# A two-layer trunk on one core: masks and gates in another memory, modulation sums taken earlier, four pooled products moved in TensorE's order, and the first attention biases loaded during a feed-forward product

## The chip, the core and the metric

The kernel runs as one program on one core of a Trainium2 chip. The metric is the device time of one execution in microseconds (us). A core has five engines with a queue each: TensorE (PE, matmuls; its weight loads are listed as PEld), VectorE (DVE), ScalarE (ACT), GpSimd (POOL) and SyncE (SP), which issues all the transfers of this kernel. An engine works through its queue in order, and an instruction whose operand isn't ready holds up everything behind it on its engine.

## The reference

512 tokens of 1024 features go through two layers of two steps each; a step is x + gate * norm(fn(norm(x) * (1 + scale) + shift)). The three modulation vectors of a step come from silu(c) times a matrix (`ada_w`).

```python
def sandwich(x, mod, g_pre, g_post, fn):
    shift, scale, gate = mod
    h = rms_norm(x, g_pre) * (1.0 + scale[:, None]) + shift[:, None]
    return x + gate[:, None] * rms_norm(fn(h), g_post)
...
for layer in range(DEPTH):
    # layer 0: pooling and the HGRN recurrence; layer 1: dilated attention with a position bias
    x = sandwich(x, modulation(...), ..., mixer)
    x = sandwich(x, modulation(...), ..., lambda h: (silu(h @ w_a) * (h @ w_b)) @ w_out)
```

The mixer of layer 0 has two halves. The pooling half takes `u = h @ w_u` in four groups of 128 features, subtracts `u` from a running mean over 2, 4, 8 or 16 tokens, and multiplies each group by a 128x128 matrix. The HGRN half (4 heads of 128) is a gated linear recurrence over the tokens; its output is normed and multiplied by `silu(h @ w_g)`. Layer 1's attention has 24 heads in three groups, and a bias that depends on the distance of two tokens.

## The kernel before

**Arithmetic.** Every large product is made of three fp32r passes: an operand is split into a high part (`hi`, a copy by ACT, line 353 for weights and 572 for the other operand) and a low part (`lo`, a subtraction by DVE or POOL, line 286), and PE adds hi·hi, hi·lo and lo·hi (line 265, function `mm`). A weight block is 128x1024 numbers, 512 KB.

**Memory.** On-chip memory is shared out in units of 512 numbers per partition by an `Arena` each for plain data (`ar`: a zone "f" of 24 units, of which x holds 8), for temporaries (`tr`: zone "t", 8 units) and for split operands (`rr`: "r" and "o"). Two further "swing" zones, "s" and "z", belong to `ar` in the mixer and in attention and to `rr` elsewhere. The zone "o" of 4 units holds the split operands of the feed-forward output product. `get(n, zone)` takes n units of a zone, `free` gives them back; a transfer into freed units waits until their last reader is done.

**Loads.** All weight blocks stand in one list. `weights(i)` makes sure that block i is split, splits up to `ahead["split"]` blocks beyond it, and issues loads up to `ahead["load"]` blocks beyond it, as long as more than `ahead["f"]` units (and 2 for the block) of zone "f" are free. While a half is interleaved with other work (`busy`) there is no splitting ahead except where the table `ENDS` asks for it.

**Order.** PE's order is that of the program text (`hold(pe)`); in some stretches ACT, DVE, POOL and SP are held to it too, elsewhere a scheduler chooses their order when the program is built. One instruction of the modulation sums (line 405) multiplies a 128x1025 tile of `ada_w` (512.5 KB, three buffers) by silu(c) and sums it; an `ada_step` is two of them. There are 48 steps; a step's number is counted in `ada["at"]`, and the steps 8 to 19 belong to the mixer's stage.

**Stages.** Times are those of the profiled execution.

- Start (0 to 57 us): norm of x, products with `w_qf`. PE is given some products of zeros (`keep_warm`, counts in `WARM`) while it waits.
- Values (57 to about 107): `values_block(kk)`, with the first levels of the recurrence.
- Pool and gates (107 to 168): in PE's order `mixed(g)` (u), `pooled(g)` (the 128x128 product of group g, three passes, whose operand comes from `means(g)` on DVE and a split), `blocks_64`, `blocks_128` (parts of the recurrence inside 64 or 128 tokens), `gate(h)` (24 passes of 128x512 each), `keys_back`, `states`, `outputs`.
- Mixer's output product (168 to 241): `out_project(0, ...)`, in halves of 256 tokens; `between(i)` puts the rest of the recurrence (`gated_head`, `states`, `outputs`) between its blocks.
- Feed-forward of layer 0, `ffn(1, ...)` (241 to about 630): `project_head`, the rest of the 44 blocks of `w_fi`, then `out_project` over the 22 blocks of `w_fo`. Its blocks 0 to 14 are done for all 512 tokens (48 passes each), the last 7 (`tail = ENDS[1][0]`), 15 to 21, first for one half of the tokens and then for the other (24 passes each), so that the first half's norm runs beside the second half's products. `operand(i, hf)` splits the block's other operand into zone "o"; ACT and DVE can start on it once PE has read what stood there.
- Attention (from about 630), feed-forward of layer 1, output.

The 6 transfers of `load_biases(pair)` bring a pair's biases, written to memory in the mixer, into 3 units of `ar`; those of pair 0 are issued at the start of attention.

Of the kernel before, what the change touches and what calls it, by code (L numbers as in the profile page):

```python
# [51 lines left out]
WARM = 9, 5, 7  # L52
# [3 lines left out]
ADA = 12, 16  # L56
# [123 lines left out]
def trunk(ctx: ExitStack, tc: tile.TileContext, a: dict, out: bass.AP, last: int = 3):  # L180
# [275 lines left out]
    for i, b in enumerate(c_banks):  # L456
        mm(b, bk[b], small[0:1, 0:1].broadcast_to([1, P]), c_row[:, i * T : (i + 1) * T], True, True)
    warm_r = ar.get(1)
    warm = ar.ap(warm_r, P)
    pool.memset(warm, 0.0)  # L460

# [60 lines left out]
    masks_r = ar.get(3)  # L522
    masks = ar.ap(masks_r).bitcast(I32).rearrange("p (l c) -> p l c", l=6)
    for k in range(ND):
# [21 lines left out]
        if k == 6:  # L546
            sp.dma_start(ar.ap(masks_r), a["masks"])
# [215 lines left out]
    def out_project(s, base, n, srcs, ada_until, late=None):  # L763
# [79 lines left out]
        for i in range(n - tail):  # L843
# [7 lines left out]
            rr.free(g[0])  # L851
        hold(pe, act, dve, pool)
# [66 lines left out]
    acc_r = [ar.get(1) for _ in range(1)]  # L919
    accs = [ar.ap(acc_r[0])[:, pr * 256 : (pr + 1) * 256] for pr in range(2)]  # L920
    A_r = [ar.get(2, "s") for _ in range(2)]
    A = [ar.ap(r).rearrange("p (n t) -> p n t", n=8) for r in A_r]
    pool.memset(ar.ap(acc_r[0]), 0.0)
# [68 lines left out]
    if last >= 2:  # L992
        vec_r = biases()

# [137 lines left out]
    def gate(h):  # L1132
        b = bk.get()
        project(w_g + h, b)
        g_rs0.append(ar.get(1, "f"))
        act.activation(ar.ap(g_rs0[h]), bk[b], AF.Silu)
# [6 lines left out]
    def keys_back(h):  # L1143
        pr, hh = divmod(h, 2)
        if h < 2:
            kst_rs.append(tr.get(1))
            S_rs.append(tr.get(1))
# [4 lines left out]
        act.activation(tr.ap(kst_rs[h % 2], 3 * P), bk[b][:, 0 : 3 * P], AF.Copy)  # L1152
        bk.free(b)

    def states(h):

        pr, hh = divmod(h, 2)
        kst, S = tr.ap(kst_rs[h % 2], 3 * P), tr.ap(S_rs[h % 2], 3 * P)
# [14 lines left out]
    def outputs(h):  # L1173
        pr, hh = divmod(h, 2)
        S, ob = tr.ap(S_rs[h % 2], 3 * P), ob_of[h]
# [14 lines left out]
    def gated_head(h):  # L1190
# [7 lines left out]
        dve.scalar_tensor_tensor(ar.ap(y_r), bk[b], ogain, ar.ap(g_rs0[h]), ALU.mult, ALU.mult)  # L1198
# [13 lines left out]
    ar.free(acc_r[0])  # L1212
    ar.free(masks_r)
# [3 lines left out]
    pooled(1)  # L1217
    ahead.update(load=9, split=4, f=4)
    gate(0)
    both(blocks_128)  # L1220
# [5 lines left out]
    pooled(2)  # L1226
# [4 lines left out]
    pooled(3)  # L1231
    rr.free(pwh_r)
    rr.free(pwl_r)
# [12 lines left out]
    keys_back(3)  # L1246
    ada_step(ADA[1])
    out_banks = [bk.get() for _ in range(4)]

    def between(i):  # L1250
# [6 lines left out]
        elif i == 2:  # L1257
            outputs(2)
            outputs(3)
            swing_to(ar, rr)  # L1260
# [3 lines left out]
        if i < 4:  # L1264
            ada_step(20)

    def end_of_mixer():
        release()
        for r in (*qp_r, *ks_r, *A_r, v_r, *g_rs0):
            ar.free(r)  # L1270
        for r in (*t_regions, *kst_rs, *S_rs):
# [11 lines left out]
    def ffn(s, layer, ada_until, chain):  # L1283
# [31 lines left out]
        ahead.update(load=14, split=14, f=2, r=4)  # L1315
# [8 lines left out]
    def attention(s, chain):  # L1324
# [20 lines left out]
        for i in range(N_QK):  # L1345
            r = ar.get(1)
# [7 lines left out]
        biases_of = {}  # L1354

        def load_biases(pair):
            r = ar.get(3)
# [325 lines left out]
```

## Time and profile before

| what | before |
|---|---|
| median of 3 runs (lowest to highest) | 1270.33 us (1269.47 to 1273.18) |
| profiled execution, its time and its span | 1271.72 us, 1269.9 us |
| PE busy | 1231.6 us (97%) |
| DVE, ACT, POOL busy | 620.5, 461.7, 194.7 us |
| mean granted TensorE clock | 0.988 |
| transfers | 164.25 MB, mean 129 GB/s |

The span runs from the first to the last instruction; the time of the execution is a little longer. A row of the timeline gives start and duration, engine, line, operation, output and input, and in brackets how long the engine had been idle before it and what released it. PE's rows overlap by a fraction of a microsecond, since matmuls are pipelined; the distance between the starts of two rows is what counts.

### The profile page before, as it was taken

What the parts mean: (1) busy time and instruction counts of PE and PEld (TensorE: products, weight loads), DVE (VectorE), ACT (ScalarE), POOL (GpSimd) and SP (SyncE); (2) the same over time, 40 slices, a digit from 0 to 9 for tenths busy, and PEclk for the clock granted to TensorE, in tenths of its full rate; (3) what the DMA queues carried; (4) which work ended last, traced back from release to release, by engine and by line L of the source; (5) the groups of instructions that cost most, each with busy time, mean ns of one, the idle gap of its engine ahead of it and who ended that gap; (6) DMA issues with size and microseconds to landing.
All of it is one profiled execution on the core that took longest, in us unless ns stands there. A gap on an engine that the chain in (4) does not pass through costs nothing.

```text
span 1269.9 us, 20632 instructions
## 1 busy us (share of the span) xinstructions
PE 1231.6 (97%) x8672; PEld 1091.6 (86%) x8672; DVE 620.5 (49%) x974; ACT 461.7 (36%) x757; POOL 194.7 (15%) x110
## 2 busy tenths in 40 slices
PE   8999899999999999999999999999999999999997
PEld 6777699988888889998979878778998888889997
DVE  7978966754443223528485232455854222213415
ACT  4553445532222222326453233445732222222313
POOL 1000022321111111213211110022311111121002
PEclk9999899999999999999999999999999999999999
DMA  8943732336552133321378222123435222223302
GB/s 308 351 147 130 271 127 87 135 128 222 193 195 76 67 100 100 128 89 54 116 251 287 78 71 75 54 95 119 134 127 188 83 83 67 68 99 100 100 1 67
DMA packets 50383, 164.25 MB, mean 129 GB/s; under 512 B 5809, under 2 KB 11081, under 8 KB 50290
## 3 DMA queue, kind: packets, MB, share of 16 engines
q1 hardware_dynamic: 50290, 162.93, 37.8%
q8 instruction: 68, 1.11, 0.4%
q14 instruction: 25, 0.20, 0.0%
HBM read 160.78 MB, written 2.13 MB: 128 GB/s over the span
## 4 chain that ended last, share of the span: by engine, by line
PE 84%; DVE 7%; DMA 3%; ACT 2%; issue 2%; POOL 1%; SPq 0%; DVEq 0%; ACTq 0%; POOLq 0%
PE bank L265 81%; DMA ada_w<-ada 2%; DVE ada_w L405 1%; DVE r L286 1%; PE bank L1475 1%; DVE t L649 1%; PE bank L1444 1%; DVE f L653 1%; DMA f<-w_qf 1%; DVE h L688 0%; DVE t L610 0%; POOL h L286 0%; PE bank L936 0%; POOL cst L481 0%; DMA f<-w_ho 0%
## 5 line engine op out<-in xcount | busy, mean ns | idle before, releaser
L265 PE MATMUL bank<-h,r 128*128 128x512 f32 (+1 forms) x2096 | 457.5, 360 | 1.5 <-ACT h L529 0.7
L265 PEld LDWEIGHTS bank<-h,r 128*128 128x128 f32 x2096 | 358.9, 189 | 61.5 <-ACT h L529 2.0
L265 PE MATMUL bank<-h,swing 128*128 128x512 f32 (+1 forms) x1688 | 325.3, 341 | 1.2 <-DVE swing L1298 1.2
L265 PEld LDWEIGHTS bank<-h,swing 128*128 128x128 f32 x1688 | 269.9, 189 | 37.3 <-DVE swing L1298 1.4
L286 DVE TENSOR_TENSOR r<-f,r 128x1024 fp32r<-128x1024 f32 (+1 forms) x67 | 81.6, 1220 | 181.4 <-PE bank L265 98.5
L353 ACT ACTIVATE r<-f 128x1024 fp32r<-128x1024 f32 x105 | 110.3, 1058 | 140.3 <-PE bank L265 107.0
L265 PE MATMUL bank<-o,swing 128*128 128x256 f32 x1248 | 152.0, 275 | 0.0
L265 PEld LDWEIGHTS bank<-o,swing 128*128 128x128 f32 x1248 | 146.3, 188 | 0.1
L286 DVE TENSOR_TENSOR swing<-f,swing 128x1024 fp32r<-128x1024 f32 x49 | 66.3, 1357 | 133.4 <-PE bank L265 81.0
L405 DVE SCALAR_TENSOR_TENSOR ada_w<-ada_w,sil 128x1025 f32<-128x1025 f32 x96 | 126.2, 1328 | 10.3 <-DMA ada_w<-ada 9.2
L353 ACT ACTIVATE swing<-f 128x1024 fp32r<-128x1024 f32 x80 | 83.5, 1058 | 93.9 <-PE bank L265 51.5
L286 POOL TENSOR_TENSOR r<-f,r 128x1024 fp32r<-128x1024 f32 x24 | 58.7, 2445 | 323.6 <-PE bank L265 243.7
L265 PE MATMUL bank<-o,r 128*128 128x256 f32 x864 | 107.4, 276 | 0.0
L265 PEld LDWEIGHTS bank<-o,r 128*128 128x128 f32 x864 | 102.6, 188 | 0.2
L1297 ACT ACTIVATE t<-bank 128x512 f32<-128x512 f32 (+1 forms) x52 | 27.2, 531 | 176.2 <-PE bank L265 176.0
L286 POOL TENSOR_TENSOR swing<-f,swing 128x1024 fp32r<-128x1024 f32 x23 | 56.6, 2460 | 215.2 <-PE bank L265 175.5
L265 PE MATMUL bank<-h,o 128*128 128x512 f32 (+1 forms) x296 | 78.2, 350 | 1.7 <-DVE h L688 1.7
L265 PE MATMUL bank<-r,h 128*128 128x512 f32 x288 | 73.4, 404 | 0.6 <-ACT swing L907 0.6
L265 PEld LDWEIGHTS bank<-r,h 128*128 128x128 f32 x288 | 62.5, 252 | 8.1 <-ACT swing L913 1.2
L286 DVE TENSOR_TENSOR o<-f,o 128x256 fp32r<-128x256 f32 (+2 forms) x38 | 26.6, 717 | 73.7 <-ACT o L572 66.8
L265 PEld LDWEIGHTS bank<-h,o 128*128 128x128 f32 x296 | 52.6, 190 | 10.0 <-DVE h L688 2.1
L481 POOL TENSOR_TENSOR cst<-cst 128x2 f32<-128x2 f32 (+1 forms) x19 | 16.9, 891 | 275.8 <-DVE cst L479 275.8
(189 smaller groups left out, 1005.9 us busy)
## 6 DMA issues: line engine op xcount, KB each, us to landing
ada_w<-ada SPq DMA_DIRECT2D x96, 512.5 KB, 4.7
f<-w_fi SPq DMA_DIRECT2D x88, 512.0 KB, 4.5
f<-w_fo SPq DMA_DIRECT2D x44, 512.0 KB, 3.4
f<-w_aqk SPq DMA_DIRECT2D x24, 512.0 KB, 4.5
f<-w_av SPq DMA_DIRECT2D x12, 512.0 KB, 3.9
f<-w_qf SPq DMA_DIRECT2D x8, 512.0 KB, 7.2
f<-w_ho SPq DMA_DIRECT2D x8, 512.0 KB, 4.0
f<-x SPq DMA_DIRECT2D x8, 256.0 KB, 4.5
```

The costliest lines, as they stand in the source:

```text
L265: i = pe.matmul(o, lhsT, rhs, start=start, stop=stop, skip_group_check=True)
L286: eng.tensor_tensor(o, x, y, ALU.subtract)
L353: act.activation(hi, w, AF.Copy)
L405: return dve.scalar_tensor_tensor(w, w, 1.0, sil, ALU.mult, ALU.mult, accum_out=mods[:, s, 2 * j + k : 2 * j + k + 1])
L481: newest_rstd[0] = pool.tensor_tensor(r, v, mhalf[:, 0:cols], ALU.pow).ins.name
L649: dve.tensor_tensor(us[i], us[i], rows, ALU.mult)
L653: (pool if i < 2 else dve).tensor_tensor(x, x, us[i], ALU.add)
L1297: act.activation(tr.ap(sa)[:, cols], a, AF.Silu)
L1444: pe.matmul(o, qc, kc, start=True, stop=True, skip_group_check=True)
L1475: pe.transpose(bk[b][:, seg * P : (seg + 1) * P], sc[:, i * P : (i + 1) * P], ident)
```

## The change

1. **Zones.** The masks (3 units), their accumulators (1 unit) and the four gates (1 unit each) move from zone "f" to the temporaries "t"; the four tiles of `keys_back` and `states` move from "t" to the swing zone "z". Attention's first six query and key tiles must lie in zone "s".
2. **Modulation sums.** The four values blocks take 2, 2, 1 and 1 steps (before 1 each): steps 8 to 13 there, not 8 to 11. One step is taken among the gates (before four), and five between the blocks of the output product (before four).
3. **Order of the pooled products.** `pooled(1)` moves behind `gate(0)`, `pooled(2)` behind `gate(2)`, `pooled(3)` behind `gate(3)`, `outputs` and `keys_back`.
4. **Zeros.** Four products of zeros are multiplied ahead of those that spread c (`PREWARM`), and 13 in place of 9 at the first `keep_warm`.
5. **First biases.** `load_biases(0)` goes from the start of attention to the point behind block 14 of `w_fo` in the feed-forward of layer 0. So that there is room, the reserve `ahead["f"]` is 8 units (before 2) in that product up to this point, and 2 from there on.

```diff
-WARM = 9, 5, 7
+PREWARM = 4
+WARM = 13, 5, 7
...
-ADA = 12, 16
+ADA = 14, 15
...
+    for _ in range(PREWARM):
+        mm(c_banks[1], bk[c_banks[1]][:, 0:P], warm, warm, True, True)
     for i, b in enumerate(c_banks):
...
-    masks_r = ar.get(3)
+    masks_r = tr.get(3)
...
             weights_done(base + i)
             rr.free(g[0])
+            if s == 1 and last >= 2 and i == n - tail - 1:
+                load_biases(0)
+                ahead.update(f=2)
...
-    acc_r = [ar.get(1) for _ in range(1)]
+    acc_r = [tr.get(1) for _ in range(1)]
...
+    def load_biases(pair):
+        r = ar.get(3, None if pair else "f")
...
         values_block(kk)
-        ada_step(ADA[0])
+        for _ in range(2 - kk // 2):
+            ada_step(ADA[0])
...
-        g_rs0.append(ar.get(1, "f"))
+        g_rs0.append(tr.get(1))
...
-            kst_rs.append(tr.get(1))
-            S_rs.append(tr.get(1))
+            kst_rs.append(ar.get(1, "z"))
+            S_rs.append(ar.get(1, "z"))
...
     means(2)
-    pooled(1)
     ahead.update(load=9, split=4, f=4)
     gate(0)
+    pooled(1)
     both(blocks_128)
...
     gate(1)
-    pooled(2)
     keys_back(0)
     keys_back(1)
     ada_step(ADA[1])
     gate(2)
-    pooled(3)
-    rr.free(pwh_r)
-    rr.free(pwl_r)
+    pooled(2)
     states(0)
     states(1)
...
     outputs(1)
     keys_back(2)
     keys_back(3)
+    pooled(3)
+    rr.free(pwh_r)
+    rr.free(pwl_r)
     ada_step(ADA[1])
...
         if i < 4:
             ada_step(20)
+        if i == 3:
+            ada_step(20)
...
-        ahead.update(load=14, split=14, f=2, r=4)
+        ahead.update(load=14, split=14, f=8 if s == 1 else 2, r=4)
         return out_project(s, w_fo[layer], NF, g_rs, ada_until)
...
-            r = ar.get(1)
+            r = ar.get(1, "s")
...
-        load_biases(0)
```

**PE in the mixer, before:** from the last pass of `gate(0)` (first row) over `blocks_128` (64x64), `gate(1)` (x24), `pooled(2)` (r,o x3), two `keys_back`, `gate(2)` and `pooled(3)` to the first `states`. `pooled(1)` stands ahead of `gate(0)`.

```order
L265 MATMUL bank_79<-h,o 128x512
L1125 MATMUL bank_81<-swing_0_87,swing_1_88 64x64 x8
L1125 MATMUL bank_74<-swing_0_87,swing_1_88 64x64 x8
L265 MATMUL bank_75<-h,r 128x512 x24
L265 MATMUL bank_76<-r,o 128x512 x3
L1151 MATMUL bank_77<-cst,swing_1_88 128x128 x3
L1151 MATMUL bank_78<-cst,swing_1_88 128x128 x3
L265 MATMUL bank_80<-h,r 128x512 x24
L265 MATMUL bank_79<-r,o 128x512 x3
L265 MATMUL bank_81<-swing_3_90,t 128x128 x3
```

The same place after, with lines that are a little higher:

```order
L266 MATMUL bank_80<-h,o 128x512
L266 MATMUL bank_79<-r,o 128x512 x3
L1141 MATMUL bank_81<-swing_0_87,swing_1_88 64x64 x8
L1141 MATMUL bank_74<-swing_0_87,swing_1_88 64x64 x8
L266 MATMUL bank_75<-h,r 128x512 x24
L1167 MATMUL bank_76<-cst,swing_1_88 128x128 x3
L1167 MATMUL bank_77<-cst,swing_1_88 128x128 x3
L266 MATMUL bank_78<-h,r 128x512 x24
L266 MATMUL bank_80<-r,o 128x512 x3
L266 MATMUL bank_79<-swing_3_90,swing_2_96 128x128 x3
```

Each of the three `r,o` products now has a gate of 24 passes, or more, between itself and the place where it stood.

**ACT at the end of the `w_fo` blocks, before.** `L353 ... 128x1024` is the high part of a weight block; `L572 o<-f` is the high part of the other operand, 128x512 for blocks up to 14 and 128x256 for one half's blocks from 15 on. The splits into `swing_2_1821` and `swing_3_1822` are attention's already.

```order
L353 ACTIVATE swing_0_4357<-f 128x1024
L353 ACTIVATE swing_1_4358<-f 128x1024
L572 ACTIVATE o<-f 128x512
L353 ACTIVATE swing_2_4359<-f 128x1024
L353 ACTIVATE swing_0_1819<-f 128x1024
L572 ACTIVATE o<-f 128x512
L353 ACTIVATE swing_1_1820<-f 128x1024
L353 ACTIVATE swing_2_1821<-f 128x1024
L572 ACTIVATE o<-f 128x512
L572 ACTIVATE o<-f 128x256 x2
L353 ACTIVATE swing_3_1822<-f 128x1024
L572 ACTIVATE o<-f 128x256 x6
```

The same engine and place after; `swing_3_1832` is block 15 of `w_fo`, the two `r<-f` pairs are 16, 17 and 18, 19, `swing_0_1829` and `swing_1_1830` are 20 and 21, the last two are attention's.

```order
L575 ACTIVATE o<-f 128x256 x2
L354 ACTIVATE swing_3_1832<-f 128x1024
L575 ACTIVATE o<-f 128x256
L354 ACTIVATE r<-f 128x1024 x2
L575 ACTIVATE o<-f 128x256
L354 ACTIVATE r<-f 128x1024 x2
L575 ACTIVATE o<-f 128x256
L354 ACTIVATE swing_0_1829<-f 128x1024
L354 ACTIVATE swing_1_1830<-f 128x1024
L575 ACTIVATE o<-f 128x256
L354 ACTIVATE swing_2_1831<-f 128x1024
L354 ACTIVATE swing_0_4348<-f 128x1024
```

The weight splits of blocks 16 to 21, which all stood ahead of the half's operands, now stand between them, two by two.

**SP's transfers there, after** (before, 22 of `w_fo` stood in one row, then 6 of `w_aqk`, 4 of `w_av`, and the 6 of `row`):

```order
L329 DMA f<-w_fo 128x1024 x14
L1007 DMA f<-row_524 32x2x259 x4
L329 DMA f<-w_fo 128x1024
L1007 DMA f<-row_527 128x2x128
L1007 DMA f<-row_530 128x2x128
L329 DMA f<-w_fo 128x1024 x7
L329 DMA f<-w_aqk 128x1024 x6
```

The six transfers of the biases are now ahead of block 14's and block 15's weights.

More of the change, by code (lines that the diff above doesn't have):

```diff
@@ L546, in trunk @@
         if k == 6:
-            sp.dma_start(ar.ap(masks_r), a["masks"])
+            sp.dma_start(tr.ap(masks_r), a["masks"])
         passes = ((hi, h_hi), (lo, h_hi), (hi, h_lo))
@@ L1211, in trunk @@
     both(weights_32)
-    ar.free(acc_r[0])
-    ar.free(masks_r)
+    tr.free(acc_r[0])
+    tr.free(masks_r)
     mixed(3)
@@ L1259, in between @@
             outputs(3)
+            for r in (*kst_rs, *S_rs):
+                ar.free(r)
             swing_to(ar, rr)
```

38 lines of the change are left out of this document (18 added, 20 removed).

## The prediction

> **What bounds the kernel now.** I read first the busy times, the slices and the summary of the chain on the profile's page.
>
> ```profile
> PE 1231.6 (97%) x8672; PEld 1091.6 (86%) x8672; DVE 620.5 (49%) x974; ACT 461.7 (36%) x757; POOL 194.7 (15%) x110
> PEclk9999899999999999999999999999999999999999
> PE 84%; DVE 7%; DMA 3%; ACT 2%; issue 2%; POOL 1%; SPq 0%; DVEq 0%; ACTq 0%; POOLq 0%
> ```
>
> PE carries the end. The change adds only eight small matmuls to it, so what it can win or lose is PE's idle time and the stretches at a lower clock: 1269.9 less 1231.6 is 38 us of the one, and the fifth slice shows the other. The table by windows (per engine busy time and count, then clock, transfer share, GB/s) says where they lie.
>
> ```profile
> 57.00:120.00 63.00, 62.12 (x990) 48.59 (x991) 48.03 (x94) 27.52 (x42) 0.37 (x3) 0.97 0.47 166
> 120.00:160.00 40.00, 31.93 (x213) 25.62 (x212) 36.90 (x61) 20.86 (x34) 0.00 (x0) 0.83 0.71 252
> 550.00:570.00 20.00, 20.00 (x179) 20.00 (x178) 4.09 (x10) 4.54 (x10) 0.00 (x0) 1.00 0.14 42
> 632.00:645.00 13.00, 10.97 (x90) 8.29 (x89) 9.75 (x20) 7.46 (x14) 2.38 (x1) 0.87 0.63 185
> ```
>
> Between 120 and 160 us PE is idle for 8.1 us at a mean clock of 0.83, with DVE busy for 36.9 of 40: a place where the change can win. At 550 to 570, in the `w_fo` product's last blocks, PE is full at full clock: there it can only lose. PE's timeline shows the first in single rows.
>
> ```profile
> 122.16 0.70 PE L1114 MATMUL bank<-swing,swing 128*32 128x32 f32 x32 [0.53 <-DVE swing L948]
> 123.59 0.50 PE L265 MATMUL bank<-r,o 128*128 128x512 f32 x1 [0.74 <-ACT r L572]
> 125.19 1.22 PE L265 MATMUL bank<-r,o 128*128 128x512 f32 x2 [1.09 <-DVE r L286]
> 126.20 1.05 PE L265 MATMUL bank<-h,r 128*128 128x512 f32 x2
> 136.14 5.75 PE L265 MATMUL bank<-h,r 128*128 128x512 f32 x24
> 152.96 0.80 PE L265 MATMUL bank<-r,o 128*128 128x512 f32 x1 [4.26 <-ACT r L572]
> 155.22 1.22 PE L265 MATMUL bank<-r,o 128*128 128x512 f32 x2 [1.46 <-DVE r L286]
> 156.23 1.49 PE L265 MATMUL bank<-swing,t 128*128 128x128 f32 x6
> 158.85 0.83 PE L265 MATMUL bank<-swing,t 128*128 128x128 f32 x6
> 167.92 3.11 PE L265 MATMUL bank<-h,r 128*128 128x256 f32 x24
> 171.41 0.91 PE L265 MATMUL bank<-swing,t 128*128 128x128 f32 x6
> 172.96 3.11 PE L265 MATMUL bank<-h,r 128*128 128x256 f32 x24
> ```
>
> The `r,o` rows are `pooled(1)` and `pooled(3)`: PE stands at each twice, for the high and for the low part of an operand that DVE's `means` finishes late. After each pause the matmuls are slow.
>
> **Part 1, the mixer (changes 1, 2, 3).** `pooled(1)` costs 0.74 + 1.09 us idle, and slow passes:
>
> ```profile
> 125.19 9.02 PE bank L265 x26
> 150.92 1.23 DVE L405 SCALAR_TENSOR_TENSOR ada_w<-ada_w,sil 128x1025 f32<-128x1025 f32 x1 [0.54 <-DMA ada_w<-ada]
> 154.48 0.68 DVE L286 TENSOR_TENSOR r<-f,r 128x512 fp32r<-128x512 f32 x1
> ```
>
> 26 passes took 9.02 us (chain of waits); at 5.75 / 24 = 0.24 us each they would take 6.2, so 2.8 us went to the clock. `pooled(3)` costs 4.26 + 1.46 idle. From 155.22 its two passes and the first `states` (14 small passes) take 1.01 and 2.62 us; at full clock two passes take 0.48 and the second-half `states` (171.41 to 172.96) 1.55: 1.6 us to the clock. Sum 0.74 + 1.09 + 2.8 + 4.26 + 1.46 + 1.6 = 12.0 us.
>
> After, each pooled product stands behind at least 24 passes (5.75 us) more than its wait was, and DVE has six modulation halves less before `pooled(3)`'s low part (154.48 there, just behind such halves): they run in the values stage, whose window has DVE idle for 15 of 63 us and PE idle for 0.9. The new order, laid along DVE's and ACT's queues with these rows' durations, starts the output product at about 154.4 where it was 167.92. That is 13.5 us early, of which a part comes back: `pooled(3)` itself (0.7 us) merely moved, and three small waits arise, since DVE now has five steps between the blocks: 0.9 us for the bank that the normed output of head 0 frees, 0.4 at the first `gated_head`, 1.2 where block 4's weight split on ACT now stands behind the squares of `outputs(2)` and `outputs(3)`. I take 12.0 - 2.5 = **9.5 us gained**, with bounds of 12 (no new wait) and 6: from 131 to 157 us some 15 transfers of half a megabyte are due, 7.7 MB in 26 us or 300 GB/s, more than the 252 that this stretch moved, and each tile that lands late holds DVE's queue, `states` and heads behind it. One wait of 4.26, as DVE's lateness cost here, would leave about 6.
>
> The zone moves issue no instruction of their own. The masks' transfer stays one transfer.
>
> **Part 2, the start (change 4).** PE's timeline there:
>
> ```profile
> 3.26 3.77 PE L265 MATMUL bank<-t,cst 1*128 1x512 f32 x4 [3.26 <-ACT t L454]
> 6.96 4.21 PE L265 MATMUL bank<-f 128*128 128x128 f32 x18
> 11.56 1.09 PE L265 MATMUL bank<-cst,t 128*128 128x1 f32 x8 [0.38 <-DVE t L497]
> 17.16 5.86 PE L265 MATMUL bank<-h,o 128*128 128x512 f32 x24
> ```
>
> The first four zeros fit into the 3.26 us in which PE waits for c. The other four are 8 passes of 4.21 / 18 = 0.23, 1.9 us, where 0.38 is idle ahead of the sums of squares; with PE warmer by then, passes may halve. The products at 17.16 already run at full speed (24 in 5.86). Bounds: +1.5 (all of it delays the sums and the norm behind them) and -0.3. I take 0: DVE's first modulation half, which the scale behind the norm needs too, starts only at 11.75, released by its transfer.
>
> ```profile
> 11.75 1.23 DVE L405 SCALAR_TENSOR_TENSOR ada_w<-ada_w,sil 128x1025 f32<-128x1025 f32 x1 [0.24 <-DMA ada_w<-ada]
> ```
>
> **Part 3, the `w_fo` product (change 5).** SP's and DVE's timelines, and groups and transfers of the page:
>
> ```profile
> 415.64 114.69 SPq L328 DMA_DIRECT2D f<-w_fo  x22
> 531.60 17.92 SPq L328 DMA_DIRECT2D f<-w_aqk  x6
> 556.62 0.42 DVE L286 TENSOR_TENSOR o<-f,o 128x256 fp32r<-128x256 f32 x1 [2.29 <-ACT o L572]
> 559.34 0.42 DVE L286 TENSOR_TENSOR o<-f,o 128x256 fp32r<-128x256 f32 x1 [2.29 <-ACT o L572]
> L286 DVE TENSOR_TENSOR r<-f,r 128x1024 fp32r<-128x1024 f32 (+1 forms) x67 | 81.6, 1220 | 181.4 <-PE bank L265 98.5
> L353 ACT ACTIVATE r<-f 128x1024 fp32r<-128x1024 f32 x105 | 110.3, 1058 | 140.3 <-PE bank L265 107.0
> L286 POOL TENSOR_TENSOR r<-f,r 128x1024 fp32r<-128x1024 f32 x24 | 58.7, 2445 | 323.6 <-PE bank L265 243.7
> f<-w_fo SPq DMA_DIRECT2D x44, 512.0 KB, 3.4
> f<-w_aqk SPq DMA_DIRECT2D x24, 512.0 KB, 4.5
> ```
>
> Before, all 22 loads are issued by 530.3 and the weights split long ahead; in the tail only the operand's half is split (DVE every 2.72 us, the price of a half-block of 24 passes), and PE never stands. After, the reserve lets no load run ahead, and ACT takes the weight splits of blocks 16 to 21 between operands that must wait for PE, since each new operand takes the place in "o" of one that PE is just reading. From T, PE's end of block 15:
>
> - Block 16: ACT's operand (17's, free only at T), 0.42 us as DVE's row of that size, then the weights' high part, 1.06, then POOL's low part, 2.45: ready at T + 3.9, PE stands for 3.8.
> - Block 18: its load goes into the units that this low part frees: 3.9 + 3.4 (landing) + 1.06 + 2.45 = 10.8. Blocks 16 and 17 have ended by 3.9 + 5.2 = 9.1: PE stands for 1.7.
> - Block 20: the same round again, 10.8 + 3.4 + 1.06 + 2.45 = 17.7, and its operand comes behind the high part of 21's weights and DVE's low part of it, at about 18.2, where PE is done at 10.8 + 5.2 = 16.0: 2.2.
> - Block 21: its operand stands on ACT behind two `w_aqk` splits, whose loads wait for the low parts of 20 and 21 (18): 18 + 3.4 to 4.5 + 2 x 1.06 + 0.42 + 0.42, and 0 to 1.2 for a split ahead of it on DVE: 24.4 to 26.7, where PE is done at 20.7: some 4.3.
>
> Sum 12.0. PE's idle stretches drop its clock: the window 632 to 645, with one pause of 2.03 us in it (below), ran at 0.87, which is 13 x 0.13 / 0.5 = 3.4 us at half speed, 1.7 lost. Slow passes of blocks 16 to 20 only shorten the next wait, since that is set by transfers and splits; those behind block 21 count in full: 1.7. Together **13.7 us lost**. Blocks 0 to 14 keep ahead by 1 to 2 us each in the same reckoning; the biases' six transfers, 7.17 us on SP where they were, now delay block 15's weights:
>
> ```profile
> 601.29 7.17 SPq L1361 DMA_DIRECT2D f<-row  x6
> 632.36 2.38 DVE L286 TENSOR_TENSOR r<-f,r 128x1024 fp32r<-128x1024 f32 x2 [13.54 <-issue]
> 635.13 5.98 PE L265 MATMUL bank<-o,h 128*128 128x512 f32 x18 [2.03 <-DVE swing L1342]
> ```
>
> Those weights still come about 1 us early: nothing. Bounds for the tail: 6 (blocks 16 and 20 alone, if the rest hides) and 19 (both bounds of block 21's operand and four falls of the clock). I take 13.7, since each step is a row of this trace.
>
> **Part 4, attention's start.** PE waits 2.03 us for copies on DVE that stand behind two weight splits (2.38); in the new order only one is ahead: 1.2 saved, and 2.9 if the clock then holds. The biases' transfers before it released nobody. I take **2**.
>
> **Sum.** 13.7 - 9.5 - 2 + 0 = 2.2 us slower: 1273.9 against the profiled execution's own 1271.7. That execution is 1.4 above the median of the runs, so against the median, 1270.33 + 2.2 = **1272.5**. Less than 0.3% (3.8 us) either way can hardly be told from no change.
>
> **Rivals.**
>
> 1. *The tail hides its splits.* Block 16's load may land early and POOL's low part be wanted only at the third pass; were the waits at 16, 18 and 20 covered like those of blocks 5 to 15, the loss would be 1 to 2 us: 1270.3 - 9.5 - 2 + 1.5 = 1260.3, to 1258 with the whole 12. For it: at 531 to 550 the old order too has splits beside 256-wide operands, without a stop. Against: those loads were on chip by then. It decides if block 16's high part on ACT ends before PE ends block 15.
> 2. *The mixer gives its gain back* (slower): DVE's modulation halves wait for tiles, and the recurrence's outputs, queued behind them, stop the output product, as the 0.54 and 4.26 above already show. At 300 GB/s due, a backlog of 3 to 4 us on each of two heads leaves 1 to 2 us of the gain: 1270.3 + 13.7 - 2 - 1.5 = 1280.5. It decides if DVE's idle time "<-DMA ada_w" between 130 and 160 passes some 4 us.
> 3. *The clock falls at more of the tail's waits and stays down*, as at 125 to 131, where three pauses of 0.53 to 1.09 within 3 us cost 2.8: two more such stretches, 2 x 2.8: 1278.
>  [...]
>
> **How the numbers follow.** The sum as worked, with mixer 6 to 12, tail 11 to 16 and attention 1.2 to 2.9, 1266 to 1279: 0.49, of it 0.05 below 1266.5, 0.28 within 0.3% and 0.16 above 1274.1. Rival 1: 0.29, 0.27 of it faster, 0.02 same. Rival 2: 0.12, slower but for 0.01. Rival 3: 0.10, slower but for 0.01. Sums: faster 0.32, same 0.32, slower 0.36. The range takes in rival 1's lower end and rival 2's time: 1258 to 1281.
>
> **What would show it.** Right: PE's rows `r,o` without idle ahead, the output product's first block near 154 to 156, no slow stretch between 120 and 160; in the `w_fo` product's second part PE rows `bank<-o,...` with idle time released by ACT and POOL, four of them, the last the longest, and a clock below 1 there; attention's first copies one split earlier. Wrong: a full PE row through the tail (rival 1), DVE idle for modulation tiles and PE waiting at `gated_head` (rival 2), or a clock near 0.8 over more than 7 us of the tail (rival 3). If blocks before 15 already wait for weights, the loss is larger than any case here.

## The result, and the profile after

| | before | after |
|---|---|---|
| median (lowest to highest), 4 runs each | 1269.9 us (1265.22 to 1273.18) | 1288.64 us (1286.44 to 1289.56) |
| profiled execution, time and span | 1271.72, 1269.9 us | 1286.44, 1284.7 us |

The ratio after to before is 1.0148, 95% interval 1.0113 to 1.0183: 18.7 us slower. The forecast was 1272.5, range 1258 to 1281: the sign of the likeliest case was right, the size far off, and the time lies outside the range. The profiled execution is the fastest of its four, so the traces account for 14.8 us of it.

The page after, busy times and the summary of the chain:

```profile
PE 1236.7 (96%) x8688; PEld 1096.7 (85%) x8688; DVE 619.1 (48%) x976; ACT 460.8 (36%) x757; POOL 190.5 (15%) x108
PE 81%; DVE 8%; DMA 4%; ACT 3%; issue 3%; POOL 1%; SPq 0%; DVEq 0%; ACTq 0%; POOLq 0%
```

PE has 48.0 us idle (1284.7 less 1236.7) where it had 38.3. The table by windows says where they now lie; the first four stretches are those of the prediction, the fifth is the whole tail.

```profile
57.00:120.00 63.00, 60.34 (x980) 46.95 (x981) 51.48 (x101) 27.70 (x41) 0.37 (x3) 0.97 0.56 194
120.00:160.00 40.00, 38.79 (x285) 32.85 (x283) 37.61 (x69) 24.62 (x55) 2.76 (x2) 1.00 0.70 237
550.00:570.00 20.00, 14.18 (x95) 13.58 (x95) 6.08 (x5) 5.04 (x7) 5.01 (x3) 0.83 0.34 106
632.00:645.00 13.00, 13.00 (x100) 13.00 (x100) 7.88 (x17) 6.46 (x13) 2.49 (x1) 0.89 0.50 172
545.00:590.00 45.00, 30.04 (x191) 28.35 (x190) 15.91 (x17) 14.24 (x24) 9.42 (x4) 0.81 0.36 117
```

Between 120 and 160 us PE gained what was hoped: 38.8 busy at full clock, where it was 31.9 at 0.83. The `w_fo` tail lost more than that: in 545 to 590 PE is busy for 30 of 45 us at a clock of 0.81, while DVE, ACT, POOL and the transfers all have time to spare. That is the mark of a chain in which each waits for the other.

Where the difference arises, by the starts of the same instructions in both traces:

| place | before | after | sum of the difference |
|---|---|---|---|
| first `blocks_64` pass | 120.93 | 123.07 | +2.1 |
| mixer's output product starts | 167.92 | 156.49 | -11.4 |
| its first half ends | 197.33 | 191.53 | -5.8 |
| block 15 of `w_fo` ends | 553.45 | 547.53 | -5.9 |
| last bank of the tail's first half | 569.76 | 587.51 | +17.8 |
| attention's first scores | 641.04 | 657.99 | +17.0 |
| end of the span | 1269.9 | 1284.7 | +14.8 |

The tail alone is 16.3 us before and 40.0 after. PE's timeline there (in brackets the idle time ahead of a row; `bank<-o,r` are blocks 16 to 19, `bank<-o,swing` 20 and 21):

```profile
548.95 0.50 PE L266 MATMUL bank<-o,r 128*128 128x256 f32 x2 [1.45 <-ACT r L354]
551.43 5.52 PE L266 MATMUL bank<-o,r 128*128 128x256 f32 x46 [1.98 <-POOL r L287]
558.77 0.50 PE L266 MATMUL bank<-o,r 128*128 128x256 f32 x2 [1.82 <-ACT r L354]
561.20 5.49 PE L266 MATMUL bank<-o,r 128*128 128x256 f32 x24 [1.93 <-POOL r L287]
569.94 0.38 PE L266 MATMUL bank<-o,swing 128*128 128x256 f32 x1 [0.64 <-ACT o L575]
572.55 4.51 PE L266 MATMUL bank<-o,swing 128*128 128x256 f32 x23 [2.23 <-DVE o L287]
579.70 0.39 PE L266 MATMUL bank<-o,swing 128*128 128x256 f32 x1 [2.64 <-ACT o L575]
582.35 7.33 PE L266 MATMUL bank<-o,swing 128*128 128x256 f32 x42 [2.27 <-DVE o L287]
```

Four places, as forecast, at blocks 16, 18, 20 and 21, with two waits each: together 14.96 us. The passes tell the clock: 46 in 5.52 us at 551 (0.12 each), 24 in 5.49 at 561 (0.23 each), which is half speed. Half speed (a clock of 0.50) was granted for 17 us in all, from 559.9, 573.5 and 580.3; PE worked in 13.7 of them, so the slow passes cost some 6.9. 14.96 + 6.9 make up 21.8 of the 23.7 by which the tail is longer. The rest is about what eight stops cost at some 0.25 us each, an estimate: the two passes at 548.95 take 0.50, where 46 in 5.52 make 0.24 for two.

What sets a round of the tail is in the chain of waits:

```profile
549.87 2.59 DVE r L287
...
552.49 0.33 SPq L329
...
552.90 4.73 DMA f<-w_fo
...
558.62 1.05 ACT r L354
...
559.75 2.48 DVE swing L287
562.23 0.35 DVE o L287
...
562.68 4.82 DMA f<-w_fo
```

DVE's low part frees the units of a block, SP sends the next loads, they land after 4.7 to 4.8 us, ACT makes the high parts of both (the second ends after 2.0), DVE the second's low part: from the one load's 552.90 to the next one's 562.68, 9.8 us. It adds up from the chain: 4.73 for the landing, 0.98 and 1.05 for the two high parts, 2.48 and 0.35 on DVE (the weights' low part and, behind it, an operand's), and 0.2 between them. PE multiplies two blocks in 5.4 (2 x 2.72).

### The profile page after: what moved, and what is told of

It is laid out like the page before. It is cut to its first block, busy times and chain, and to the rows that moved or that the text cites. A ratio compares the mean times of both kernels' runs of the same rounds, so it can differ in the third digit from the quotient of the medians.

```text
span 1284.7 us, 20668 instructions
## 1 busy us (share of the span) xinstructions
PE 1236.7 (96%) x8688; PEld 1096.7 (85%) x8688; DVE 619.1 (48%) x976; ACT 460.8 (36%) x757; POOL 190.5 (15%) x108
## 4 chain that ended last, share of the span: by engine, by line
PE 81%; DVE 8%; DMA 4%; ACT 3%; issue 3%; POOL 1%; SPq 0%; DVEq 0%; ACTq 0%; POOLq 0%
PE bank L266 78%; DVE swing L287 1%; DMA ada_w<-ada 1%; DVE ada_w L406 1%; PE bank L1485 1%; DVE r L287 1%; DVE h L691 1%; DVE t L652 1%; PE bank L1454 1%; DMA f<-w_fo 1%; PE bank L942 1%; DMA f<-w_qf 1%; DVE f L656 1%; ACT t L643 1%; DMA f<-w_v 0%
## 5 line engine op out<-in xcount | busy, mean ns | idle before, releaser
L266 PE MATMUL bank<-h,r 128*128 128x512 f32 (+1 forms) x2024 | 441.9, 361 | 5.0 <-DVE h L691 1.7
L266 PEld LDWEIGHTS bank<-h,r 128*128 128x128 f32 x2024 | 346.4, 189 | 65.1 <-ACT h L532 2.7
L266 PE MATMUL bank<-h,swing 128*128 128x512 f32 (+1 forms) x1784 | 336.5, 339 | 4.3 <-DVE h L287 1.3
L266 PEld LDWEIGHTS bank<-h,swing 128*128 128x128 f32 x1784 | 281.4, 190 | 40.9 <-DVE swing L1318 1.6
L266 PE MATMUL bank<-o,swing 128*128 128x256 f32 x1248 | 157.1, 280 | 7.8 <-DVE o L287 4.5
L266 PEld LDWEIGHTS bank<-o,swing 128*128 128x128 f32 x1248 | 150.5, 192 | 8.7 <-DVE o L287 4.9
L287 DVE TENSOR_TENSOR r<-f,r 128x1024 fp32r<-128x1024 f32 x66 | 84.0, 1274 | 148.6 <-PE bank L266 86.9
L406 DVE SCALAR_TENSOR_TENSOR ada_w<-ada_w,sil 128x1025 f32<-128x1025 f32 x96 | 124.8, 1309 | 10.8 <-DMA ada_w<-ada 9.5
L287 POOL TENSOR_TENSOR swing<-f,swing 128x1024 fp32r<-128x1024 f32 x25 | 62.0, 2479 | 238.2 <-PE bank L266 160.2
L266 PE MATMUL bank<-h,o 128*128 128x512 f32 (+1 forms) x272 | 73.1, 356 | 0.0
L266 PEld LDWEIGHTS bank<-h,o 128*128 128x128 f32 x272 | 48.5, 188 | 8.1 <-ACT h L532 0.2
```

The costliest lines, as they stand in the source:

```text
L266: i = pe.matmul(o, lhsT, rhs, start=start, stop=stop, skip_group_check=True)
L287: eng.tensor_tensor(o, x, y, ALU.subtract)
L406: return dve.scalar_tensor_tensor(w, w, 1.0, sil, ALU.mult, ALU.mult, accum_out=mods[:, s, 2 * j + k : 2 * j + k + 1])
```

## The experiments

The ratios are to the kernel before on the same chip, whose median there was 1270 to 1274. Two questions come first: which part costs the time, and what in it.

**Part 5 taken out, and part 5 alone.** The first run leaves `load_biases(0)` and the reserve as before the change, in the kernel after; the second makes that change alone, in the kernel before.

```diff
-            if s == 1 and last >= 2 and i == n - tail - 1:
-                load_biases(0)
-                ahead.update(f=2)
-        ahead.update(load=14, split=14, f=8 if s == 1 else 2, r=4)
+        ahead.update(load=14, split=14, f=2, r=4)
```

> The changed kernel without its part 5 (no reserve of 8 units, first biases back at the start of attention); everything else as changed. Theory A (all of the loss is made in the last blocks of w_fo, by the missing look-ahead): the tail runs without waits as before, and what is left is the mixer's gain, 5.8 us in the trace, less or more 2 at attention's start: 0.995 to 0.998 of before, about 1264 us. Rival B (part of the 15 to 19 us comes from the zones, the sums or the order in the mixer): 1268 or more.

Measured: 1266.72 us (1261.44 to 1270.23), ratio 0.9954 (0.993 to 0.9978), and no wait in the tail. Parts 1 to 4 are thus worth some 6 us, and part 5 costs 22 to 25 beside them (22 by the medians, which are from two chips, 25 by the ratios).

> The kernel before with part 5 alone. Theory A: tail waits as in the changed kernel, 23 us, less some 4 us at attention's start: 1.013 to 1.019, about 1289 us. Rival B: well under 1285.

Measured: 1295.86 us, ratio 1.0202 (1.0176 to 1.0227), just above what was expected, with the waits of the kernel after in its tail and those of the kernel before in its mixer. The two halves of the change work apart from each other.

**Reserve without room.** The reserve of 8 stays, but the biases go back to attention's start, so that they hold no units in the tail.

> The changed kernel with the reserve of 8 units kept up to block 14 of w_fo, but the first biases loaded at the start of attention: no row transfers among the weights, and 3 units more of zone f for the tail. Theory A1 (the reserve alone is the cause, since it takes away the look-ahead; the transfers of the biases cost nothing): the waits at blocks 16 to 21 stay, at most one round shorter: 1280 to 1290. Rival A2 (the six row transfers ahead of the weights, and the room that they take, are the cause): 1262 to 1267.

Measured: 1271.23 us, ratio 0.999 (0.9973 to 1.0007), in neither of the two ranges expected; the tail takes 24.8 us. PE's timeline has only the first round's two waits in full:

```profile
549.83 0.50 PE L266 MATMUL bank<-o,r 128*128 128x256 f32 x2 [1.45 <-ACT r L354]
552.32 11.03 PE L266 MATMUL bank<-o,r 128*128 128x256 f32 x71 [1.99 <-POOL r L287]
```

and ACT splits three blocks at once where the kernel after had two (`x2` at 547.85):

```profile
548.74 2.93 ACT L354 ACTIVATE r<-f 128x1024 fp32r<-128x1024 f32 x3
```

So the reserve alone costs about 8.5 us in the tail; the other 15 need something that comes with the biases. (The whole run is only 4.5 us slower than e1: part of the 8.5 comes back behind the tail.)

**A reserve of 4, biases as early as in the change.**

```diff
-        ahead.update(load=14, split=14, f=8 if s == 1 else 2, r=4)
+        ahead.update(load=14, split=14, f=4 if s == 1 else 2, r=4)
```

> The changed kernel with a reserve of 4 units in place of 8: the biases are loaded behind block 14 as changed, but 4 units more serve the look-ahead, and on ACT the splits of blocks 16 to 19 come ahead of the half's operands again; those of 20, 21 still stand among them. Theory A1: the rounds of 10 us are gone, at most one wait of 2 to 4 us stays: 1262 to 1268. Rival A2: the loss stays, 1280 or more.

Measured: 1265.25 us (1262.07 to 1267.75), ratio 0.9951 (0.9934 to 0.9968). The tail takes 16.5 us and PE goes through it without a stop:

```profile
550.36 8.46 PE L266 MATMUL bank<-o,swing 128*128 128x256 f32 x72
```

The early biases do no harm where the weights have run ahead. They do no good that shows either: e1, without them, has 0.9954.

**Room or transfers?** The reserve of 8, the units taken at the same point, but the line that sends the transfers put at attention's start.

```diff
-                load_biases(0)
+                biases_of[0] = ar.get(3, "f")
...
-        r = ar.get(3, None if pair else "f")
+        r = ar.get(3) if pair else biases_of[0]
...
+        load_biases(0)
```

> The changed kernel with the reserve of 8 and with the 3 units taken out of zone f behind block 14, but nothing loaded into them there: the six transfers of the biases run at the start of attention. Theory C (what chains the loads of the tail two by two, in rounds of 10 us, is the room that the biases take while nothing is loaded ahead): as slow as the changed kernel, 1284 to 1293, with waits at blocks 16, 18, 20 and 21. Rival D (the transfers on SP's queue ahead of the weights of blocks 14 and 15 make the difference): like the reserve alone, 1267 to 1274.

Measured: 1287.46 us, ratio 1.0113 (1.0082 to 1.0145), a tail of 38.2 us. But the edit did not do what it says: SP's order is chosen when the program is built, and the trace shows the transfers at 531.95 to 539.0 as in the kernel after. A second run took the room, put the transfers into other units and gave the room back behind them:

```diff
-                load_biases(0)
+                room.append(ar.get(3, "f"))
...
+        load_biases(0)
+        ar.free(room.pop())
```

> Behind block 14 of w_fo the kernel takes the three units of zone "f" and holds them, but sends nothing there; the first pair's six bias transfers go into other units behind the 22 loads of w_fo, six of w_aqk and four of w_av, as before the change, and the held units are given back behind them at the start of attention. (In e5 the transfers, whose line stood there too, were still issued by SP at 531.95 to 539, since SP's order is chosen by the scheduler and their units were free: that run did not tell the room from the transfers.) If the room that is held makes the tail, it runs as in the kernel after: block 15's end to the last bank about 38 to 40 us, pairs of loads every 10 us, median 1285 to 1290. If the early transfers make it, by taking SP's queue and the path from memory ahead of the loads of blocks 14 to 17, the tail is that of the reserve alone, about 25 us, and the median 1270 to 1274. Something between would share it.

Measured: 1288.91 us (1287.94 to 1290.71), ratio 1.0144 (1.0108 to 1.018), a tail of 39.5 us. SP's timeline shows the loads (22, of which 12 here) in one row and the transfers `row` 61 us behind the last of them:

```profile
499.80 64.13 SPq L329 DMA_DIRECT2D f<-w_fo  x12
572.92 19.41 SPq L329 DMA_DIRECT2D f<-w_aqk  x6
592.74 27.57 SPq L329 DMA_DIRECT2D f<-w_av  x4
625.37 1.76 SPq L1008 DMA_DIRECT2D f<-row  x4
```

So the six transfers cost nothing that shows. The three units that are held, with a reserve that let nothing run ahead, are the cause: held, two blocks are loaded and split at a time (`x2` in ACT's rows); free, as in e3, three at the start.

**The clock.** Small products with zeros are added to PE's queue ahead of each wait of the tail (5, 7, 6, 7, 2, 8, 9 and 8 of them); they add zeros to the sums.

```diff
+        zeros = {(16, 0): 5, (16, 2): 7, (18, 0): 6, (18, 2): 7, (20, 0): 2, (20, 1): 8, (21, 0): 9, (21, 1): 8}
...
+                        for _ in range(zeros.get((i, n_pass), 0)):
+                            mm(b, bk[b][:, 0:P], zero, ident, False, False)
```

> The changed kernel with products of zeros on PE (0.2 us each, added to a bank, which they leave as it is) ahead of the eight places in blocks 16, 18, 20 and 21 at which PE stood for 0.6 to 2.6 us: 5 and 7, 6 and 7, 2 and 8, 9 and 8 of them. The loads and splits stay. Theory E (the clock falls because PE stands; slow passes ahead of a later wait cost nothing, those behind the last wait cost 2.4 us): no passes at half speed between 545 and 590 us, and 2 to 4 us less than the changed kernel, 1284 to 1287. Rival F (all 17 us at half speed count): 7 to 9 us less, about 1280. Rival G (zeros don't keep the clock up, or only add work): no less, or more.

Measured: 1284.61 us, ratio 1.0099 (1.0066 to 1.0132); the tail takes 36.65 us. The window of the tail:

```profile
545.00:590.00 45.00, 39.54 (x315) 37.83 (x315) 17.33 (x22) 15.88 (x28) 10.24 (x5) 0.96 0.34 120
```

The clock is 0.96 in place of 0.81, and the tail only 3.3 us shorter. So of the 6.9 us of slow passes some 3.6 only shortened the wait behind them; the round is set elsewhere.

**What makes a round.** POOL is given no low parts in this stage; DVE makes them all.

```diff
+        share[0] = 0 if s == 1 else 3
```

> The changed kernel with every low part of the w_fo product on DVE, none on POOL (2.4 us there, and DVE's own take 2.5 beside it, 1.2 alone). Theory C: a round of the tail was 5.1 to 5.3 us for two loads at a time, 1.06 for the high part, 2.4 for POOL's low part, and some 1.2 until DVE had its own done; with DVE alone 2.4 to 3 us less per round, three rounds: 6 to 9 us less than the changed kernel, 1279 to 1283. Rival H (the landing of the loads sets the round): 0 to 3 us less, 1285 to 1289.

Measured: 1278.49 us, ratio 1.0037 (1.0014 to 1.0061): 10 us won back by the medians, 14 by the ratios, and 13 in the trace's tail (27.0 us), more than expected. (The span is only 6.1 us shorter: in this trace block 15 ends 5.2 us later, for reasons ahead of the tail.) DVE's low parts take 1.23 each, and the loads no longer come in pairs. ACT's timeline shows one block at a time, waiting for single loads:

```profile
561.05 1.06 ACT L354 ACTIVATE r<-f 128x1024 fp32r<-128x1024 f32 x1 [1.22 <-DMA f<-w_fo]
564.47 1.06 ACT L354 ACTIVATE swing<-f 128x1024 fp32r<-128x1024 f32 x1 [2.05 <-DMA f<-w_fo]
567.06 1.06 ACT L354 ACTIVATE swing<-f 128x1024 fp32r<-128x1024 f32 x1 [1.53 <-DMA f<-w_fo]
```

A round, from the first block of one to the first of the next, is now 5.7 us (558.77, 564.47, 570.14), which is landing, high part and low part in a row: 3.4 + 1.06 + 1.23. With one engine for the low parts the addition of the prediction holds; with two it does not. This run takes away the pairs and POOL's part at once, so that it doesn't tell their shares apart.

**The mixer.** The other runs have the reserve of 4 of e4, so that the tail is out of the way; they are compared with its 1265.25. First, two weight splits of the feed-forward are put behind the last operands of the mixer's output product (a dependency added in `split_next`), because PE had waited 0.90 and 1.35 us for those operands:

> The kernel with the reserve of 4 (which keeps the mixer's gain and the early biases), in which the first two weight splits of the feed-forward's w_fi block come behind the mixer's last operands on ACT and DVE. In the changed kernel PE stands for 0.9 and 1.35 us at 183 to 186 for operands that stand behind weight splits on DVE. Expected: these two waits gone, 2 us less than the reserve of 4, 0.993 to 0.995 of before, 1262 to 1264. Rival: the splits are missing later, and the time is as with the reserve of 4.

Measured: 1260.8 us (1259.42 to 1263.88), ratio 0.9909 (0.9881 to 0.9937); the two waits, at 183 to 186 us, are gone. That is 4.5 us less than e4, where 2 were expected. In e4 a stretch of 3.4 us at half speed follows these waits (187.2), and here it doesn't; 1.3 us of the gain lie ahead of the edit's place (first `blocks_64` at 121.81, in e4 at 123.13).

Then the modulation sums: one step in each values block, as before, with the rest of the change to the mixer kept.

```diff
-        for _ in range(2 - kk // 2):
-            ada_step(ADA[0])
+        ada_step(ADA[0])
```

> The reserve of 4 with one modulation step per values block, as before; three steps then fall among the gates, five between the output product's blocks. Theory I (the two more steps in the values blocks are what makes that stage 2 us longer): the first pass of blocks_64 starts at 121 us, not at 123, and the time is 0 to 2 us below the reserve of 4, less what the gates lose. Rival J (something else delays the values stage): blocks_64 at 122.5 or later, and since DVE is fuller among the gates, 0 to 2 us slower.

Measured: 1269.99 us, ratio 0.9984 (0.9957 to 1.001). PE's timeline:

```profile
158.07 1.16 PE L266 MATMUL bank<-swing,swing 128*128 128x128 f32 x8 [1.69 <-DVE swing L1180]
159.06 0.82 PE L1166 MATMUL bank<-cst,swing 128*128 128x128 f32 x6
162.50 0.50 PE L266 MATMUL bank<-r,o 128*128 128x512 f32 x1 [2.62 <-ACT r L575]
```

The wait at `pooled(3)` is back, though the product stands at its new place. Theory I missed: the first `blocks_64` starts at 124.10, no earlier than with the sums moved (rival J). And the converse, the sums moved and the pooled products at their old places:

> The reserve of 4 with the four pooled products at their old places in PE's order, zones and modulation sums as changed. Theory K (the order carries the mixer's gain): PE waits again at pooled(1) and pooled(3), 1.8 us and 2 to 6 us, with half-speed passes behind: 4 to 9 us slower than the reserve of 4, about 1270. Rival L (the sums that left the gates carry it): at most 3 us slower, pooled(3) without a wait.

Measured: 1263.05 us, ratio 0.993 (0.9907 to 0.9952), and PE waits at none of the three:

```profile
123.40 0.96 PE L266 MATMUL bank<-r,o 128*128 128x512 f32 x3
137.50 0.86 PE L266 MATMUL bank<-r,o 128*128 128x512 f32 x3
144.31 0.86 PE L266 MATMUL bank<-r,o 128*128 128x512 f32 x3
```

The sums that left the gates won the mixer's time; the new order of the products added nothing. The zones (change 1) are as changed in both runs; what they do alone was not tried.

**The start.** No zeros ahead of c, and 9 at the first `keep_warm`:

> The reserve of 4 without the zeros of part 4 (none ahead of c, 9 at the first keep_warm). Theory M (the zeros themselves cost nothing, but with them the scheduler puts a weight split of w_v on ACT one pair of activations earlier, so that a bank comes free late and PE waits some 1 us at 65 to 68): the first pass of blocks_64 at 121 to 122, 0 to 2 us faster than the reserve of 4. Rival N (the zeros do help the start): 0.5 to 2 us slower, the products of the start later.

Measured: 1262.82 us, ratio 0.9925 (0.9894 to 0.9957), with the first `blocks_64` at 122.38; in e4 it is at 123.13, in the kernel after at 123.07. The zeros won nothing. In the kernel after, the products behind them start 0.5 us earlier at first (16.65 for 17.16) and are level again at 57 (57.34 for 57.29). Theory M doesn't hold as it stands: in e11 the split of `w_v` is back behind two pairs of activations on ACT (in the kernel after behind one), but PE still waits 0.95 us for them at 70.69, where it waits 0.86 at 67.97 in the kernel after.

What the traces do show is the length of the values stage, from its first `r,h` product (63.59 before) to the first `blocks_64`. It is 57.0 to 57.5 us in the four traces without the zeros (before, e2, e11, e12) and 57.6 to 60.7 in the eleven with them, wherever the modulation sums stand. Each of the eleven has a wait of 0.32 to 1.92 us near 89 (0.89 at 89.04 in the kernel after) and none of the four has it. So the zeros go with a longer values stage; what releases that wait, the traces don't show.

**What the runs point to**: reserve of 4, operands first, pooled products at their old places, no zeros.

> What the runs so far favour in one kernel: zones, modulation sums and early biases as changed, a reserve of 4, the pooled products at their old places, no zeros, and the w_fi splits behind the mixer's last operands. If the single gains add up (4 us from the splits' order, 1 to 2 each from the order of the pooled products and the start, as the ratios to before stood): 0.986 to 0.990 of before, 1255 to 1260. Rival: the pooled order and the zeros were within what the runs scatter, and the time is that of the reserve of 4 with operands first, 0.991.

Measured: 1258.67 us (1256.28 to 1261.05), ratio 0.9899 (0.9872 to 0.9926): it beats both kernels, the one after by 30 us. (The rival's 0.991 lies within the interval too, so the run doesn't tell whether the smaller gains add up.) In its table by windows the tail's stretch (550 to 570) is full again:

```profile
120.00:160.00 40.00, 38.95 (x298) 33.46 (x297) 37.45 (x69) 23.28 (x51) 3.13 (x2) 1.00 0.67 238
550.00:570.00 20.00, 19.58 (x169) 19.21 (x168) 12.23 (x24) 9.71 (x23) 3.39 (x3) 1.00 0.17 60
```

## Why the prediction was wrong

**The failed step: the round of the tail (part 3), the term of 13.7, which measured 23.7.** The mechanism was right to the block: the splits come late because the reserve lets no load run ahead, four places wait, the low part of block 16 is ready 3.9 us behind T (547.53) as worked. Then each round was counted as 3.4 + 1.06 + 2.45 = 6.9 us, and took some 10 (9.8 in the chain above). Block 18 was ready at T + 13.7 (worked 10.8), block 20 at T + 25.0 (18.2), block 21 at T + 34.8 (24.4 to 26.7). Three things were missing: the pair and DVE beside POOL, which make the round, and part of the clock's cost.

- *The pair.* The round was worked for one block on POOL. The next loads went out only at 552.49, when DVE's low part of the other block was done, though POOL's had ended 1.1 us earlier (551.37). The first of a pair landed after 3.9 us (issued at 552.49), the second after 4.7 to 4.8, not the 3.4 of the page's median; and ACT made two high parts in a row, not one. Beside the 6.9 the pair thus adds 1.3 and 1.0, and the operand on DVE 0.35.
- *DVE beside POOL.* DVE's low part was taken at 1.2 us, its mean over the kernel; beside POOL's it took 2.5 to 2.6. DVE's and POOL's rows after:

```profile
549.02 2.35 POOL L287 TENSOR_TENSOR r<-f,r 128x1024 fp32r<-128x1024 f32 x1 [21.89 <-ACT r L354]
549.87 2.58 DVE L287 TENSOR_TENSOR r<-f,r 128x1024 fp32r<-128x1024 f32 x1 [1.47 <-ACT r L354]
558.79 2.35 POOL L287 TENSOR_TENSOR r<-f,r 128x1024 fp32r<-128x1024 f32 x1 [7.42 <-ACT r L354]
559.75 2.48 DVE L287 TENSOR_TENSOR swing<-f,r 128x1024 fp32r<-128x1024 f32 x1 [4.61 <-ACT r L354]
```

  Both times DVE ends 1.08 to 1.09 us behind POOL's end (552.45 less 551.37, 562.23 less 561.14), close to its own 1.23 without POOL: it seems to stand until POOL has done. At all eleven places of the kernel after where such a low part on DVE takes over 2 us, it ends 1.08 to 1.09 behind POOL's. With 1.23 it would have been done when POOL was, and the round would be 1.1 us shorter. The trace of before showed the same, in rows that I did not read:

```profile
525.90 2.52 POOL L286 TENSOR_TENSOR swing<-f,swing 128x1024 fp32r<-128x1024 f32 x1 [0.31 <-ACT swing L353]
526.06 3.44 DVE L286 TENSOR_TENSOR swing<-f,swing 128x1024 fp32r<-128x1024 f32 x1
```

  DVE ends at 529.50, 1.08 behind POOL's 528.42. Why DVE stands there, the traces don't show; with no low parts on POOL (e7) the same low parts take DVE 1.23.
- *The clock.* 1.7 us were counted, for block 21 alone; the runs show 3.3 (e6). That the slow passes of earlier blocks only shorten the next wait was right for the rest of the 6.9.

The four waits measured 3.43, 3.75, 2.87 and 4.91 against 3.8, 1.7, 2.2 and 4.3. They look close only since the slow passes fill part of the longer rounds. And the upper bound of 19 was made from other operands and clock falls, not from a longer round, so the range did not reach the case.

**The mixer (part 1): 9.5 worked, 5.8 measured, just under the lower bound of 6.** The output product starts at 156.49 (154.4 worked), and no wait is left at the `r,o` rows, as forecast. Two smaller steps were off. The values stage ended 2.1 us later, and PE's idle time there went from 0.9 to 2.7 us. The sums moved into it are not what e9 and e12 point to: with the sums as before it ends no earlier, and with the sums moved but no zeros it ends at 120.17, ahead of the 120.93 of before. And the new small waits came to 4.7 us in place of 2.5 (these four and 0.21 at 161.48):

```profile
160.32 0.95 PE L266 MATMUL bank<-h,r 128*128 128x256 f32 x6 [1.53 <-DVE t L1203]
176.54 2.89 PE L266 MATMUL bank<-h,swing 128*128 128x256 f32 x22 [0.70 <-DVE swing L287]
184.06 0.38 PE L266 MATMUL bank<-h,swing 128*128 128x256 f32 x1 [0.90 <-ACT h L575]
185.79 5.90 PE L266 MATMUL bank<-h,swing 128*128 128x256 f32 x47 [1.35 <-DVE h L287]
```

The first is the one forecast at 0.9; the last two, which e8 takes away, were not seen. Both causes were named together in the prediction (24 passes of cover, and six sums fewer on DVE); e9 and e10 show that the second alone was needed. Rival 2, DVE waiting for tiles, was not what took the rest: the output product starts 2.1 us behind the forecast, as much as the values stage lost ahead of it, and between 130 and 160 DVE waited 2.0 us, for ACT, and for no tile.

**The start (part 2): 0 worked.** The start itself cost nothing, as said: in the kernel after the passes of zeros from 6.98 on start every 0.21 us up to 10.33 and every 0.11 behind it. But nothing was counted for what comes behind it, and the zeros go with the values stage's 2.1 us (e9, e11, e12). How much of the kernel's time that is stays open: the intervals of e11 and e4 overlap.

**Attention's start (part 4): 2 worked, 0.8 measured.** The wait of 2.03 us is gone, but a wait of 2.71 at 629, for ACT, and a stretch at half speed at 631.5 took more than half of it back: the window 632 to 645 has PE full, at a clock of 0.89.

**Rival 1**, a tail that hides its splits, fell at its own condition: the high part of block 16 begins on ACT at 547.85, behind the end of block 15 at 547.53.

**Rival 3** named the clock and gave 1278. No single gap of the tail is longer than 2.64, yet 17 us were granted at half speed. The length of the gaps does not decide it: 1.45 and 1.98 or 1.99 around 0.5 us of work stand at block 16 in the kernel after and in e2, e3, e5 and e13, and half speed follows in the last four, not in the first. The clock's stretches show what differs. In the tail after they begin and end at 559.87, 566.69, 573.52, 576.93, 580.35 and 587.17, always whole steps of 3.41 us apart. The table by windows for five such steps, the first two around the first pair (counted back from 559.87; no change of the clock marks their ends), the others just ahead of the three falls:

```profile
546.22:549.63 3.41, 1.78 (x14) 1.37 (x12) 0.42 (x1) 2.10 (x3) 0.60 (x1) 1.00 0.29 113
549.63:553.04 3.41, 1.61 (x13) 1.61 (x14) 2.58 (x1) 0.21 (x1) 1.75 (x1) 1.00 0.00 0
556.46:559.87 3.41, 0.99 (x7) 0.59 (x5) 0.12 (x1) 2.21 (x3) 1.08 (x1) 1.00 0.11 44
570.11:573.52 3.41, 1.18 (x9) 0.98 (x10) 2.39 (x2) 0.00 (x0) 0.97 (x1) 1.00 0.18 19
576.93:580.35 3.42, 0.51 (x2) 0.19 (x1) 0.98 (x1) 2.62 (x4) 1.82 (x1) 1.00 0.00 0
```

PE stood for 1.63 and 1.80 us of the first two, since the step's end counted in this way cuts the pair, and for 2.42, 2.23 and 2.91 of the others. Counted in the same way, the falls at that pair follow 2.90 us in e2, 2.32 in e3, 2.36 in e5 and 2.21 in e13, and the one stretch left in e6, at 570.0, follows 2.40. So in these tails what tells the falls from the two steps without one is the sum of the idle time within a step, 2.21 to 2.91 us against 1.63 and 1.80, not the length of a gap. It is no bound for the whole kernel: at attention's start 1.45 us in a step (from 628.1) came ahead of a fall at 631.5.

What stays open: what releases the wait near 89 us in the values stage, and 2.2 us won behind attention's scores, where a fall of the clock at 847.9 is in the trace of before and not in that of after.

## What to carry to other kernels

A reserve that stops loads from running ahead can go unnoticed until few buffers are left (here, up to the end of block 15); then load, split and freeing of the buffer form a ring, and its period, not any engine's busy time, sets the pace (here 9.8 us for two blocks that PE multiplies in 5.4). Work such a ring out for all the blocks in it at once, with the durations that instructions have beside each other (here 2.5 to 2.6 us where one alone takes 1.23) and transfers have in pairs (4.7 to 4.8 for the second, where the median is 3.4), and set the range by a longer period, not only by more of the same waits. An edit that moves a line where a scheduler chooses the order may move nothing: look for the instruction in the trace before reading the time.

## What the runs showed of the hardware

- In the tail of the kernel after a subtraction of 128x1024 took DVE 2.5 to 2.6 us when POOL had begun one of the same size 0.9 us earlier, and ended 1.08 to 1.09 behind POOL's; without POOL (e7) it took 1.22 to 1.23.
- There, of two loads of 512 KB issued 0.4 us apart the first landed after 3.9 us (issued at 552.49), the second after 4.7 to 4.8; the median of all 44 of `w_fo` is 3.4.
- PE was granted half speed (0.50) in stretches of 3.41 and 6.83 us behind gaps of at most 2.64 us each, in the tail of the kernel after; steps of 3.41 us with 2.23 to 2.91 us idle preceded the falls, two with 1.63 and 1.80, counted back from 559.87, did not.
